# Softmax weights of an attention layer: turned on VectorE and through DRAM in place of TensorE

## The chip, the core and the metric

One core of a Trainium2 chip runs the whole program. The metric is the device time of one execution, in microseconds (us). The core has five engines with a queue of instructions each: TensorE (PE; its weight loads are listed as PEld), VectorE (DVE), ScalarE (ACT), GpSimd (POOL) and SyncE (SP). Here SP does nothing but issue DMAs, and it takes them one after the other: a DMA whose condition isn't met holds up all that stand behind it.

## The reference

Two layers of the same form work on 512 rows of 1024 values. A layer normalises the rows, projects them with one wide matrix, and runs two branches over the result: an attention with 8 heads in 2 groups (compressed keys, selected blocks, window) and a gated linear attention (GLA). Both are scaled by gates, projected up, added, projected out and added to the rows.

```python
s_c = einsum(q_nope, k_cmp) * scale; p_c = masked_softmax(s_c)      # compressed keys
s_s = einsum(q_rope, k_sel) * scale; p_s = masked_softmax(s_s)      # all 8 blocks are selected at 512 rows
s_w = einsum(q_rope, k_win) * scale; p_w = masked_softmax(s_w)      # a window of 512 rows: causal
o   = g0 * (p_c @ v_cmp) + g1 * (p_s @ v_slc) + g2 * (p_w @ v_win)
o   = o * silu(z)
```

With 512 rows the selected blocks and the window both come to plain causal attention over 512 keys, with different keys and values. They are the two branches br = 0 and 1 below.

## The kernel before

Every large product is made from float32 values split in a high and a low part, with three matmuls for each block (lines 158 to 160, called `split3`). The order of TensorE's instructions is that in which the program is written; those of the other engines, and the order of the DMAs in SP's queue, are laid out by the tile framework's scheduler from its own model of the times.

The attention stage of a layer handles four pairs of heads p (head p of each group g = 0, 1). One pair has five steps: the compressed keys (`cmp_steps`), then four `attn_steps(p, ip, br)`. A unit (p, ip, br) covers the 128-row blocks of queries i = 2ip and 2ip + 1. For each i, `scores` makes the two groups' scores (line 775), and `weigh` makes weights of them: VectorE adds the mask and takes the maximum from PSUM (785), ScalarE takes the exponential (787), VectorE the reciprocal (789) and the scaling with the gate (790), into a tile of the pool "g". For i = 0 the scores of both branches are made at once. The product with the values (820) contracts over the keys, so the weights have to be turned first: TensorE transposes each 128x128 block into PSUM (808), three blocks for each group when ip = 0 and seven when ip = 1, and VectorE and ScalarE copy the banks into tiles of the pool "p" (811). The products of a pair all add into one PSUM bank (`ps_o`), which VectorE takes out at 825.

The steps are generators, and a loop written out by hand lays them on TensorE's queue: `go(n)` runs step n to its next yield, and `fill(us)` puts in between that much other work from a queue (the projections, `fm` and `up`), counted at 0.64 us for three matmuls. FILL holds the amounts by n % 5. What is left of the queue after the loop is run by `need("ug7")`; the next stage, `un`, is put in the queue only then.

The projections' weights are read by SP (line 130) into the pool "raw" of three buffers, two tiles ahead of their use, cast on ScalarE (143), and the low part is made on VectorE (144). A read waits until 144 has released a buffer.

Of the kernel before, what the change touches and what calls it, by code (L numbers as in the profile page):

```python
# [1 line left out]

# [1 line left out]

# [5 lines left out]
F32 = mybir.dt.float32  # L10
F32R = mybir.dt.float32r
# [53 lines left out]
def trunk(ctx, tc, x, wpk, sp, gvec, cs, wa, out):  # L65
    nc = tc.nc
    sb = {}

    def pool(name, bufs):
        sb[name] = ctx.enter_context(tc.tile_pool(name=name, bufs=bufs))  # L70
# [2 lines left out]
    pool("hT", 4)  # L73
    pool("hl", 6)
    pool("oT", 16)
    pool("g", 16)
    pool("a", 18)
    pool("raw", 3)
    pool("p", 12)
    pool("th", 2)  # L80
    pool("sm", 4)
    psp = {n: ctx.enter_context(tc.tile_pool(name="ps_" + n, bufs=b, space=PSUM))
# [1 line left out]
    dram = ctx.enter_context(tc.tile_pool(name="dram", bufs=1, space=bass.MemoryType.DRAM))  # L84
    cnt = [0]

    def new(pl, shape=(128, 512), dt=F32, tag=None, bufs=None):
        cnt[0] += 1
        kw = {} if bufs is None else {"bufs": bufs}
        return sb[pl].tile(list(shape), dt, tag=tag or pl, name=f"{tag or pl}_{cnt[0]}", **kw)  # L90

    def ps(tag):
        cnt[0] += 1
        return psp[tag].tile([128, 512], F32, tag=tag, name=f"ps_{tag}_{cnt[0]}")

    def const(shape, dt, name):
        return sb["const"].tile(list(shape), dt, tag=name, name=name)

    mm, tp = nc.tensor.matmul, nc.tensor.transpose
    V, A, G = nc.vector, nc.scalar, nc.gpsimd  # L100
    dma = nc.sync.dma_start


    ident = const((128, 128), F32, "ident")
# [164 lines left out]
    for l in range(L):  # L269
# [20 lines left out]
        def fill(us):  # L290
            credit[0] += us
            while credit[0] > 0.3 and queue:
                credit[0] -= step(*queue[0])
# [9 lines left out]
        def need(name):  # L303
            while name not in done:
                step(*queue[0])


        vsw = [new("a", (128, 2, 256)) for _ in range(2)]
# [63 lines left out]
        b = ps("t")  # L372
# [11 lines left out]
        for t in range(2):  # L384
            o = ps("s")
# [148 lines left out]
        PR = [[None, None, None, None] for _ in range(4)]  # L534
# [98 lines left out]
        def states(t):  # L633
            ub = [ps("s"), ps("s")]
            for n in range(7):
                rows = slice((n % 2) * 64, (n % 2) * 64 + 64)
                s = n // 2
                for r in range(2):
                    h = 2 * t + r
                    mm(ub[n % 2][r * 64:(r + 1) * 64, s * 128:(s + 1) * 128],  # L640
                       khT[t][rows, s * 128 + r * 64:s * 128 + (r + 1) * 64],
                       gv[s][rows, h * 128:(h + 1) * 128], start=True, stop=True)
            stt = [new("g", (128, 4, 128)), new("g", (128, 4, 128))]
            st.append(stt)
            for n in range(1, 8):
                u = ub[(n - 1) % 2][:, ((n - 1) // 2) * 128:((n - 1) // 2 + 1) * 128]
                d_ = stt[n // 4][:, n % 4]
                if n == 1:
                    V.tensor_copy(d_, u)
                else:  # L650
                    V.scalar_tensor_tensor(d_, stt[(n - 1) // 4][:, (n - 1) % 4], dec[t][:, n - 1:n], u,
                                           op0=OP.mult, op1=OP.add)
# [54 lines left out]
        need("gk1")  # L707
        fill(2.0)
        states(0)
        fill(1.0)  # L710
        khat_turn(1)
        fill(2.5)
        intra(0)
        fill(2.5)
        states(1)
        fill(2.5)
        intra(1)
# [41 lines left out]
            mm(acc, vbd[1], pcT, start=False, stop=False, skip_group_check=True)  # L759
            yield  # L760

        pps = {}

        def scores(p, i, brs):

            w = (i + 1) * 128
            ww = w * len(brs)
            both = len(brs) > 1  # L770
            o = [ps("s"), ps("s")]
            for g in range(2):
                for n in range(2):
                    kn = first[g][:, n].rearrange("p b n -> p (b n)") if both else keys[brs[0]][g][n][:, :w]
                    mm(o[g][:, :ww], PR[p][1][g][:, i * 128:(i + 1) * 128], kn, start=(n == 0), stop=(n == 1))  # L775
            for g in range(2):
                weigh(p, g, i, brs, o[g])

        def weigh(p, g, i, brs, o):
            h, w = p + 4 * g, (i + 1) * 128  # L780
            for n, br in enumerate(brs):
                ob = o[:, n * w:(n + 1) * w]
                sx = new("sm", (128, 4), tag="sx", bufs=8)
                pp = new("g")
                V.tensor_tensor_reduce(pp[:, :w], ob, cmask[:, 512 - w:512], 1.0, -3 * NEG,  # L785
                                       OP.add, OP.min, sx[:, 0:1])
                A.activation(pp[:, :w], pp[:, :w], AF.Exp, bias=sx[:, 0:1], scale=-1.0,  # L787
                             accum_out=sx[:, 1:2])
                V.reciprocal(sx[:, 2:3], sx[:, 1:2])
                V.tensor_scalar(pp[:, :w], pp[:, :w], sx[:, 2:3],  # L790
                                gt[:, i, h * 3 + 1 + br:h * 3 + 2 + br], op0=OP.mult, op1=OP.mult)
                pps[p, br, i, g] = pp

        def attn_steps(p, ip, br):
            for i in (2 * ip, 2 * ip + 1):
                if i or not br:
                    scores(p, i, (br,) if i else (0, 1))
                yield

            cols = [(j, i) for j in range(2 * ip + 2) for i in (2 * ip, 2 * ip + 1) if i >= j]  # L800
            pts = []
            for g in range(2):
                pt = []
                for c0 in range(0, len(cols), 4):
                    cc = cols[c0:c0 + 4]
                    bk = ps("t")
                    for n, (j, i) in enumerate(cc):
                        tp(bk[:, n * 128:(n + 1) * 128], pps[p, br, i, g][:, j * 128:(j + 1) * 128], ident)  # L808
                    pt.append(new("p"))
                    w = len(cc) * 128  # L810
                    (A.copy if (g + c0 // 4) % 2 else V.tensor_copy)(pt[-1][:, :w], bk[:, :w])  # L811
                pts.append(pt)
                yield
            acc = PR[p][3]
            for j in range(2 * ip + 2):
                n = cols.index((j, max(j, 2 * ip)))
                w = 256 if j <= 2 * ip else 128
                for g in range(2):
                    c0 = br * 128 + g * 64
                    mm(acc[g * 64:(g + 1) * 64, (2 * ip + 2) * 128 - w:(2 * ip + 2) * 128],  # L820
                       vsw[j // 2][:, j % 2, c0:c0 + 64], pts[g][n // 4][:, n % 4 * 128:n % 4 * 128 + w],
                       start=False, stop=(br == 1 and j == 2 * ip + 1), skip_group_check=True)
            if ip == 1 and br == 1:
                f_ = new("p")
                V.scalar_tensor_tensor(f_, acc, 0.5, PR[p][2], op0=OP.mult, op1=OP.mult)
                H, Lo = new("oT", dt=F32R), new("oT", dt=F32R)
                A.copy(H, f_)  # L827
                G.tensor_tensor(Lo, f_, H.bitcast(F32), op=OP.subtract)  # L828
                oTn[p] = (H, Lo)
            yield  # L830

        steps = []
# [5 lines left out]
        def go(n):  # L838
            if 0 <= n < len(steps):
                next(live[n])  # L840


        for n in range(len(steps) + 2):
            m = n % 5
            f4 = FILL[m]
            if n < len(steps):
                if m == 0:
                    need(f"q{steps[n][0]}")
                if m == 4:
                    need(f"nz{steps[n][0]}")  # L850
            go(n)
            if m in (1, 4):
                go(n - 3)
                go(n - 2)
            fill(f4[0])
            if m != 1:
                go(n - 1)
            fill(f4[1])
            if m != 0:
                go(n)  # L860
                fill(f4[2])
            if m == 2:
                go(n - 2)
            go(n - 1)
            fill(f4[3])
        need("ug7")

# [2 lines left out]
        def take_un(f):  # L870
            def g(th, u):
                t_ = new("p")
                V.scalar_tensor_tensor(t_, th, 1.0, u, op0=OP.add, op1=OP.mult)
                G.tensor_tensor(t_, t_, y2[f], op=OP.add)
                H, Lo = new("g", dt=F32R), new("g", dt=F32R)
                A.mul(H, t_, 0.5)
                V.scalar_tensor_tensor(Lo, t_, 0.5, H.bitcast(F32), op0=OP.mult, op1=OP.subtract)
                yT.append((H, Lo))
            return g
# [13 lines left out]
        for s in range(ST):  # L893
# [4 lines left out]
            o = [ps("s" if s % 2 and n < 2 else "mm") for n in range(len(pieces))]  # L898
# [100 lines left out]
```

## Time and profile before

| | |
|---|---|
| median of 3 runs | 843.58 us (843.55 to 844.6) |
| the profiled execution | 843.52 us, its span 841.7 us |
| TensorE busy | 819.9 us, 97% of the span |
| VectorE busy | 544.4 us, 65% |
| ScalarE busy | 374.9 us, 45% |
| GpSimd busy | 94.9 us, 11% |
| moved by DMA | 82.62 MB |

All times inside the execution are counted from the first instruction of the span. The execution's own time is 1.8 us longer than its span. The attention stage of the first layer lies from 147.0 us (scores of the compressed keys, p = 0) to about 316 us (the last product with the values), that of the second layer from 556.2 us.

### The profile page before, as it was taken

The page shows a single profiled execution, that of the slowest core. Times are in us where ns is not written, and L with a number is a line of the kernel's source. Part 1 is how long each engine was busy: PE and PEld are TensorE (multiplying, and loading weights), DVE is VectorE, ACT ScalarE, POOL GpSimd, SP SyncE. Part 2 cuts the span into 40 slices and gives each one's busy share as a digit, 9 for nine tenths or more (in the row PEclk, how much of TensorE's full clock was granted, in tenths as well). Part 3 has the DMA queues.
Part 4 walks back from the last instruction along what each step waited for, and adds up shares of the span by engine and source line. Part 5 has one row for each costly group of instructions (what it writes and reads, how often), then busy time and mean ns, then how long its engine had stood idle before and what let it go on. Part 6 is the DMA issues. An engine that isn't in the chain of part 4 may idle for free.

```text
span 841.7 us, 12316 instructions
## 1 busy us (share of the span) xinstructions
PE 819.9 (97%) x4570; PEld 676.8 (80%) x4570; DVE 544.4 (65%) x1192; ACT 374.9 (45%) x775; POOL 94.9 (11%) x118
## 2 busy tenths in 40 slices
PE   4999999999999999999999999999999999999996
PEld 3888788888888878888898878887888888788886
DVE  5653749987776755655564465699877767366322
ACT  4681236564544544443256412555554545244211
POOL 3110033001000001121010001410100000112100
PEclk9999999999999999999999999999999999999999
DMA  8432124221122123546246121332121212255321
GB/s 287 163 135 78 51 67 122 75 70 51 52 63 66 60 63 101 165 157 221 72 136 210 50 76 51 104 96 78 51 63 52 63 51 64 75 154 160 125 100 51
DMA packets 31515, 82.62 MB, mean 98 GB/s; under 512 B 4032, under 2 KB 4576, under 8 KB 31456
## 3 DMA queue, kind: packets, MB, share of 16 engines
q1 hardware_dynamic: 31456, 81.84, 31.1%
q8 instruction: 36, 0.59, 0.3%
q14 instruction: 23, 0.19, 0.1%
HBM read 74.48 MB, written 4.19 MB: 93 GB/s over the span
## 4 chain that ended last, share of the span: by engine, by line
PE 92%; DVE 4%; issue 2%; DMA 1%; SPq 1%; POOL 0%; POOLq 0%; ACT 0%; DVEq 0%; ACTq 0%
PE ps_mm L158 22%; PE ps_mm L160 21%; PE ps_mm L159 21%; PE ps_o L820 4%; PE ps_s L775 4%; PE ps_t L808 4%; PE ps_mm L905 2%; PE ps_mm L906 2%; PE ps_mm L908 2%; PE ps_s L908 1%; PE ps_s L905 1%; PE ps_s L906 1%; DVE a L452 1%; PE ps_mm L467 1%; PE ps_t L207 1%
## 5 line engine op out<-in xcount | busy, mean ns | idle before, releaser
L158 PE MATMUL ps_mm<-hT,hl 128*128 128x512 f32 x544 | 221.2, 407 | 0.0
L159 PE MATMUL ps_mm<-hT,hl 128*128 128x512 f32 x544 | 212.8, 391 | 0.0
L160 PE MATMUL ps_mm<-hT,hl 128*128 128x512 f32 x544 | 212.5, 391 | 0.0
L143 ACT CAST hl<-raw 128x1024 fp32r<-128x1024 f32 (+3 forms) x110 | 100.5, 915 | 145.0 <-PE ps_mm L159 105.1
L144 DVE TENSOR_TENSOR hl<-raw,hl 128x1024 fp32r<-128x1024 f32 (+3 forms) x109 | 128.2, 1178 | 48.3 <-ACT hl L143 46.5
L160 PEld LDWEIGHTS ps_mm<-hT,hl 128*128 128x128 f32 x544 | 102.2, 188 | 22.6
L158 PEld LDWEIGHTS ps_mm<-hT,hl 128*128 128x128 f32 x544 | 102.3, 188 | 20.7 <-issue 2.1
L159 PEld LDWEIGHTS ps_mm<-hT,hl 128*128 128x128 f32 x544 | 102.5, 188 | 17.7
L787 ACT ACTIVATE g<-g,sx 128x128 f32<-128x128 f32 (+3 forms) x128 | 70.8, 554 | 66.9 <-DVE sx L785 66.4
L785 DVE CUSTOM_DVE_ANT_0 g<-ps_s,cmask 128x128 f32<-128x128 f32 (+3 forms) x128 | 57.5, 487 | 28.9 <-PE ps_s L775 28.6
L790 DVE TENSOR_SCALAR g<-g,sx,gt 128x128 f32<-128x128 f32 (+3 forms) x128 | 57.7, 461 | 2.8
L158 PE MATMUL ps_mm<-oT,hl 128*128 128x512 f32 x128 | 52.7, 412 | 0.0
L159 PE MATMUL ps_mm<-oT,hl 128*128 128x512 f32 x128 | 50.1, 391 | 0.0
L160 PE MATMUL ps_mm<-oT,hl 128*128 128x512 f32 x128 | 50.0, 391 | 0.0
L808 PEld LDWEIGHTS ps_t<-ident,g 128*128 128x128 f32 x320 | 38.7, 140 | 9.6 <-DVE g L790 1.4
L775 PE MATMUL ps_s<-a,a 128*128 128x256 f32 (+2 forms) x224 | 46.4, 329 | 0.0
L808 PE MATMUL ps_t<-ident,g 128*128 128x128 f32 x320 | 45.7, 272 | 0.7 <-DVE g L790 0.7
L775 PEld LDWEIGHTS ps_s<-a,a 128*128 128x128 f32 x224 | 38.3, 188 | 6.0
L181 POOL TENSOR_TENSOR rs<-ms,mhalf 128x1 f32<-128x1 f32 (+1 forms) x24 | 17.7, 738 | 205.0 <-DVE ms L179 201.1
L811 ACT COPY p<-ps_t 128x384 f32<-128x384 f32 (+1 forms) x48 | 24.4, 507 | 34.2 <-PE ps_t L808 34.0
L828 POOL TENSOR_TENSOR oT<-p,oT 128x512 fp32r<-128x512 f32 x8 | 12.4, 1555 | 240.6 <-ACT oT L827 240.6
L820 PE MATMUL ps_o<-p,a 128*64 128x256 f32 (+1 forms) x384 | 38.1, 348 | 0.0
(225 smaller groups left out, 1343.5 us busy)
## 6 DMA issues: line engine op xcount, KB each, us to landing
raw<-wpk SPq DMA_DIRECT2D x96, 512.0 KB, 3.5
raw<-wpk SPq DMA_DIRECT2D x32, 256.0 KB, 2.7
a<-wpk SPq DMA_DIRECT2D x16, 256.0 KB, 4.6
p<-x SPq DMA_DIRECT2D x16, 256.0 KB, 4.0
g<-x SPq DMA_DIRECT2D x8, 256.0 KB, 5.5
p<-gvec SPq DMA_DIRECT2D x8, 256.0 KB, 6.0
p<-a SPq DMA_DIRECT2D x32, 64.0 KB, 2.0
x<-p SPq DMA_DIRECT2D x8, 256.0 KB, 2.0
```

The costliest lines, as they stand in the source:

```text
L143: A.copy(H[:, :w], r[:, :w])
L144: (G if i == 1 else V).tensor_tensor(Lo[:, :w], r[:, :w], H[:, :w].bitcast(F32), op=OP.subtract)
L158: mm(o, w[0], h[0], start=first, stop=False)
L159: mm(o, w[0], h[1], start=False, stop=False)
L160: mm(o, w[1], h[0], start=False, stop=last)
L775: mm(o[g][:, :ww], PR[p][1][g][:, i * 128:(i + 1) * 128], kn, start=(n == 0), stop=(n == 1))
L785: V.tensor_tensor_reduce(pp[:, :w], ob, cmask[:, 512 - w:512], 1.0, -3 * NEG, OP.add, OP.min, sx[:, 0:1])
L787: A.activation(pp[:, :w], pp[:, :w], AF.Exp, bias=sx[:, 0:1], scale=-1.0, accum_out=sx[:, 1:2])
L790: V.tensor_scalar(pp[:, :w], pp[:, :w], sx[:, 2:3], gt[:, i, h * 3 + 1 + br:h * 3 + 2 + br], op0=OP.mult, op1=OP.mult)
L808: tp(bk[:, n * 128:(n + 1) * 128], pps[p, br, i, g][:, j * 128:(j + 1) * 128], ident)
L820: mm(acc[g * 64:(g + 1) * 64, (2 * ip + 2) * 128 - w:(2 * ip + 2) * 128], vsw[j // 2][:, j % 2, c0:c0 + 64], pts[g][n // 4][:, n % 4 * 128 ...
L905: mm(o[n][:, :c1 - c0], yy[0], wo[k][h][0][:, c0:c1], start=(k == 0), stop=False)
```

## The change

The transposes on TensorE and the copies out of PSUM go. In their place, `turn` has VectorE transpose the weights in blocks of 32x32, one instruction for each i and group, into a tile T of 128 x 4 x r values (r = 192 for ip = 0 and 448 for ip = 1, so 384 KB and 896 KB). When both i of a unit are there, the tile is written to DRAM by one DMA and read back by four, each of which puts a quarter onto 32 partitions of a tile W. The products take their moving operand from W, in runs of 32 values. T has one buffer for each ip, W two. Each unit's write is ordered behind the last read of the unit before in SP's queue. The pools "g" and "p" lose four buffers each; the GLA states and three of the pairs that `un` makes live in the buffers of W and T.

The products with the values move later: those of ip = 0 from the next steps to the end of step m = 4 (m = n % 5), those of ip = 1 from the start of the next pair's m = 1 to the start of its m = 2. The loop has one more turn at its end. FILL is unchanged.

```diff
-    pool("g", 16)
+    pool("g", 12)
-    pool("p", 12)
+    pool("p", 8)
+    pool("T", 1)
+    pool("PT", 2)
...
-            stt = [new("g", (128, 4, 128)), new("g", (128, 4, 128))]
+            both = new("PT", (128, 2, 4, 128), tag="PT1")
+            stt = [both[:, 0], both[:, 1]]
...
+        PT, TT, held, back = {}, {}, {}, []
+        def turn(p, br, i, pps):
+            ip, n = i // 2, i + 1
+            r = (4 * ip + 3) * 64
+            if i % 2 == 0:
+                TT[p, br] = new("T", (128, 4, r), tag=f"T{ip}")
+            T = TT[p, br]
+            t = T[:, :, (i % 2) * i * 64:((i % 2) * i + n) * 64].rearrange("p b (j g q) -> p b j g q", j=n, g=2)
+            for g in range(2):
+                V.transpose(t[:, :, :, g], pps[g][:, :n * 128].rearrange("p (j b q) -> p b j q", j=n, b=4))
+            if i % 2:
+                cnt[0] += 1
+                dr = dram.tile([128, 4, r], F32, tag=f"tp{ip}", name=f"tp_{cnt[0]}", bufs=2)
+                with tc.issue_after(back[-1]) if back else nullcontext():
+                    dma(dr, T)
+                W = PT[p, br, ip] = new("PT", (128, 4, r), tag=f"PT{ip}")
+                for b in range(4):
+                    back.append(dma(W[b * 32:(b + 1) * 32], dr[:, b].rearrange("(a k) r -> k a r", a=4)).ins)
...
-            cols = [(j, i) for j in range(2 * ip + 2) for i in (2 * ip, 2 * ip + 1) if i >= j]
...
-                        tp(bk[:, n * 128:(n + 1) * 128], pps[p, br, i, g][:, j * 128:(j + 1) * 128], ident)
...
-                    (A.copy if (g + c0 // 4) % 2 else V.tensor_copy)(pt[-1][:, :w], bk[:, :w])
...
+                    if j <= i0:
+                        m = W[:, :, :2 * (i0 + 1) * 64].rearrange("p a (i j g q) -> p i a j g q", i=2, g=2, q=32)
+                        m, w = m[:, :, :, j, g], 256
+                    else:
+                        m, w = W[:, :, (2 * j) * 64 + g * 32:(2 * j) * 64 + g * 32 + 32], 128
...
-        for n in range(len(steps) + 2):
+        for n in range(len(steps) + 3):
...
             go(n)
-            if m in (1, 4):
+            if m == 2:
+                go(n - 4)
                 go(n - 3)
-                go(n - 2)
             fill(f4[0])
-            if m != 1:
+            if m == 1:
                 go(n - 1)
             fill(f4[1])
...
             if m == 2:
                 go(n - 2)
-            go(n - 1)
+            if m == 4:
+                go(n - 3)
+                go(n - 2)
             fill(f4[3])
...
-                H, Lo = new("g", dt=F32R), new("g", dt=F32R)
+                if f < 3:
+                    both = new("PT", (128, 2, 512), F32R, tag="PT1") if f < 2 else new("T", (128, 2, 512), F32R, tag="T1")
+                    H, Lo = both[:, 0], both[:, 1]
+                else:
+                    H, Lo = new("g", dt=F32R), new("g", dt=F32R)
```

## Rows read from the trace of the kernel before

**Rows 1.** The page's busy times (part 1) and its chain of waits (part 4).

```profile
span 841.7 us, 12316 instructions
PE 819.9 (97%) x4570; PEld 676.8 (80%) x4570; DVE 544.4 (65%) x1192; ACT 374.9 (45%) x775; POOL 94.9 (11%) x118
...
PE 92%; DVE 4%; issue 2%; DMA 1%; SPq 1%; POOL 0%; POOLq 0%; ACT 0%; DVEq 0%; ACTq 0%
```

**Rows 2.** Windows of layer 0's attention: length, busy us per engine, clock, DMA share, GB/s.

```profile
147.00:182.80 35.80, 35.47 (x192) 29.10 (x190) 33.22 (x90) 21.26 (x52) 2.59 (x2) 1.00 0.25 70
182.80:223.80 41.00, 41.00 (x241) 33.37 (x241) 32.14 (x94) 21.63 (x55) 3.21 (x2) 1.00 0.20 58
223.80:264.70 40.90, 40.90 (x241) 33.31 (x241) 30.88 (x91) 20.49 (x51) 1.81 (x1) 1.00 0.20 59
264.70:303.00 38.30, 38.30 (x225) 31.29 (x225) 26.82 (x82) 17.96 (x45) 1.81 (x1) 1.00 0.21 62
303.00:316.00 13.00, 13.00 (x86) 10.22 (x85) 6.12 (x14) 4.07 (x9) 0.00 (x0) 1.00 0.21 62
```

**Rows 3.** Timeline of TensorE around seven transposes: start, duration, instruction.

```profile
218.11 0.39 PE L159 MATMUL ps_mm<-oT,hl 128*128 128x512 f32 x1
218.34 0.40 PE L160 MATMUL ps_mm<-oT,hl 128*128 128x512 f32 x1
218.57 0.93 PE L808 MATMUL ps_t<-ident,g 128*128 128x128 f32 x7
219.25 0.48 PE L158 MATMUL ps_mm<-oT,hl 128*128 128x512 f32 x1
```

**Rows 4.** Groups of instructions by line and shape: busy us, mean ns, idle before.

```profile
L808 PE MATMUL ps_t<-ident,g 128*128 128x128 f32 x320 | 45.7, 272 | 0.7 <-DVE g L790 0.7
...
L785 DVE CUSTOM_DVE_ANT_0 g<-ps_s,cmask 128x512 f32<-128x512 f32 x32 | 20.8, 687 | 1.8 <-PE ps_s L775 1.6
...
L785 DVE CUSTOM_DVE_ANT_0 g<-ps_s,cmask 128x384 f32<-128x384 f32 x32 | 16.6, 554 | 11.4 <-PE ps_s L775 11.4
...
L785 DVE CUSTOM_DVE_ANT_0 g<-ps_s,cmask 128x256 f32<-128x256 f32 x32 | 12.4, 420 | 8.0 <-PE ps_s L775 8.0
...
L785 DVE CUSTOM_DVE_ANT_0 g<-ps_s,cmask 128x128 f32<-128x128 f32 x32 | 7.8, 286 | 7.7 <-PE ps_s L775 7.7
```

**Rows 5.** The five windows of rows 2 for line 811 alone: their sum.

```profile
sum 169.00, DVE 14.29 ACT 12.18; mean DVE 2.86 ACT 2.44
```

**Rows 6.** DMA issues (part 6): size of one, median us from issue to landing.

```profile
raw<-wpk SPq DMA_DIRECT2D x96, 512.0 KB, 3.5
raw<-wpk SPq DMA_DIRECT2D x32, 256.0 KB, 2.7
...
p<-a SPq DMA_DIRECT2D x32, 64.0 KB, 2.0
```

**Rows 7.** Line 506 (DMAs onto 32 partitions) in SP's queue: ns min/median/max of one issue.

```profile
L506 SPq DMA_DIRECT2D p<-a x32: 512/586/1526, 136.1 to 600.6; - x32
```

**Rows 8.** Timeline of TensorE at the end of layer 0's attention.

```profile
301.89 1.07 PE L775 MATMUL ps_s<-a,a 128*128 128x512 f32 x4
...
312.05 3.25 PE L820 MATMUL ps_o<-p,a 128*64 128x256 f32 x32
...
316.72 0.39 PE L158 MATMUL ps_mm<-hT,hl 128*128 128x512 f32 x1
```

**Rows 9.** The chain of waits in order of time: the last products of ip = 0.

```profile
296.87 1.45 PE ps_o L820 x16
```

**Rows 10.** Timeline of VectorE: the last scaled weights of layer 0.

```profile
305.64 0.99 DVE L790 TENSOR_SCALAR g<-g,sx,gt 128x512 f32<-128x512 f32 x2
```

**Rows 11.** Timeline of TensorE: last scores of p = 1, first transposes of p = 2.

```profile
220.03 1.07 PE L775 MATMUL ps_s<-a,a 128*128 128x512 f32 x4
...
241.49 0.49 PE L808 MATMUL ps_t<-ident,g 128*128 128x128 f32 x3
```

**Rows 12.** What SP's queue waited for: us in total, times, longest.

```profile
SPq L130 <- DVE hl L144: 384.0, 75, 18.4
```

More of the change, by code (lines that the diff above doesn't have):

```diff
@@ L1 @@
-from contextlib import ExitStack
+from contextlib import ExitStack, nullcontext
 import numpy as np
@@ L760, in cmp_steps @@
             yield
-        pps = {}
+        PT, TT, held, back = {}, {}, {}, []
[16 more added lines that the diff above has]
+                    back.append(dma(W[b * 32:(b + 1) * 32], dr[:, b].rearrange("(a k) r -> k a r", a=4)).ins)
         def scores(p, i, brs):
@@ L775, in scores @@
                     mm(o[g][:, :ww], PR[p][1][g][:, i * 128:(i + 1) * 128], kn, start=(n == 0), stop=(n == 1))
-            for g in range(2):
-                weigh(p, g, i, brs, o[g])
+            pps = [weigh(p, g, i, brs, o[g]) for g in range(2)]
+            turn(p, brs[0], i, [t[0] for t in pps])
+            if both:
+                held[p] = [t[1] for t in pps]
         def weigh(p, g, i, brs, o):
             h, w = p + 4 * g, (i + 1) * 128
+            out = []
             for n, br in enumerate(brs):
@@ L791, in weigh @@
                                 gt[:, i, h * 3 + 1 + br:h * 3 + 2 + br], op0=OP.mult, op1=OP.mult)
-                pps[p, br, i, g] = pp
+                out.append(pp)
+            return out
         def attn_steps(p, ip, br):
@@ L797, in attn_steps @@
                     scores(p, i, (br,) if i else (0, 1))
+                else:
+                    turn(p, br, i, held.pop(p))
                 yield
-            cols = [(j, i) for j in range(2 * ip + 2) for i in (2 * ip, 2 * ip + 1) if i >= j]
[L801 to L807, printed above, removed]
-                        tp(bk[:, n * 128:(n + 1) * 128], pps[p, br, i, g][:, j * 128:(j + 1) * 128], ident)
-                    pt.append(new("p"))
-                    w = len(cc) * 128
-                    (A.copy if (g + c0 // 4) % 2 else V.tensor_copy)(pt[-1][:, :w], bk[:, :w])
[L812 to L817, printed above, removed]
+            acc, W = PR[p][3], PT[p, br, ip]
+            i0 = 2 * ip
+            for j in range(i0 + 2):
                 for g in range(2):
                     c0 = br * 128 + g * 64
-                    mm(acc[g * 64:(g + 1) * 64, (2 * ip + 2) * 128 - w:(2 * ip + 2) * 128],
-                       vsw[j // 2][:, j % 2, c0:c0 + 64], pts[g][n // 4][:, n % 4 * 128:n % 4 * 128 + w],
-                       start=False, stop=(br == 1 and j == 2 * ip + 1), skip_group_check=True)
+                    if j <= i0:
[3 more added lines that the diff above has]
+                        m, w = W[:, :, (2 * j) * 64 + g * 32:(2 * j) * 64 + g * 32 + 32], 128
+                    mm(acc[g * 64:(g + 1) * 64, (i0 + 2) * 128 - w:(i0 + 2) * 128],
+                       vsw[j // 2][:, j % 2, c0:c0 + 64], m,
+                       start=False, stop=(br == 1 and j == i0 + 1), skip_group_check=True)
             if ip == 1 and br == 1:
@@ L874, in g @@
                 G.tensor_tensor(t_, t_, y2[f], op=OP.add)
-                H, Lo = new("g", dt=F32R), new("g", dt=F32R)
+                if f < 3:
+                    both = new("PT", (128, 2, 512), F32R, tag="PT1") if f < 2 else new("T", (128, 2, 512), F32R, tag="T1")
+                    H, Lo = both[:, 0], both[:, 1]
+                else:
+                    H, Lo = new("g", dt=F32R), new("g", dt=F32R)
                 A.mul(H, t_, 0.5)
@@ L990 @@
     arrays = {k: np.ascontiguousarray(v) for k, v in _layout(inputs).items()}
-    nc = _bacc.Bacc("TRN2", target_bir_lowering=False, num_devices=1)
+    nc = _bacc.Bacc("TRN2", target_bir_lowering=False, num_devices=1, dynamic_dma_scratch_size=1024)
     args = [nc.dram_tensor(n, arrays[n].shape, mybir.dt.from_np(arrays[n].dtype), kind="ExternalInput").ap()
```

## The prediction

> **What bounds the kernel now.** I read the busy times first. TensorE is busy for 97% of the span, and the chain of waits that ended last runs through it for 92% [rows 1]. A busy TensorE need not be full, so I cut the first layer's attention stage into its four pairs of heads and the end. In these windows TensorE has no gap at all but 0.3 us in the first, at a granted clock of 1.00 [rows 2]: every instruction taken off its queue there shortens the stage, as long as nothing else becomes late. What could become late stands in the same rows: VectorE is busy for 33.2 of 35.8 us in the first pair, for 26.8 to 32.1 us in the others, and for 129.2 of 169.0 us in all five windows. The DMA engines are at a quarter of their time or less.
>
> **TensorE's share.** A transpose's own row says 272 ns, but they overlap [rows 4]. What one is worth is read from the timeline. The matmul ahead of a group of seven ends at 218.34 + 0.40 = 218.74, the one behind it at 219.25 + 0.48 = 219.73. That one matmul is worth 0.23 us, the distance of the two starts ahead (218.11, 218.34) [rows 3], so the seven took 0.99 - 0.23 = 0.76 us, 0.109 each. For 320 of them it is **34.9 us** off the queue, 17.4 in each layer. The stretch of rows 2 would fall from 169.0 to 151.6 us if TensorE stayed full. The products with the values keep their number and columns. Their operand now comes in runs of 32 values; no row shows such a read. It can hardly gain, as the columns stay, and if it ran at half speed it would cost the products' own time once more: 1.45 us for a pair's ip = 0 and 3.25 for its ip = 1 [rows 8, 9], 4.7 x 8 = 38 us. I take nothing, since no column is added.
>
> **VectorE's share.** Copies out of PSUM go: 14.3 us in the stretch [rows 5]. ScalarE's copies go too, 12.2 us, and give nothing, since ScalarE was half idle. In their place come 64 transposes in a layer, 16 of each width from 128 to 512. None is in the trace. The nearest row by shape and rate is the masking at line 785, which passes one value a step: 286, 420, 554 and 687 ns [rows 4]. 16 x 1.947 = 31.2 us. Lower end: the cost of a wide one grows half as fast, 24.7 us; upper end: every 128-column block pays the price of a 128-wide instruction, 160 x 0.286 = 45.8 us. I take 31.2, since the width has a clear slope in the rows. Then VectorE's work in the stretch is 129.2 - 14.3 + 31.2 = 146.1 us. That is under TensorE's 151.6, but the most that VectorE has reached in a window of this stage is 33.2 / 35.8 = 0.93 [rows 2], as it also waits inside each softmax for ScalarE. At 0.93, 146.1 us of work need 157.4 us. VectorE, not TensorE, then sets the stretch: 5.8 us of the gain are given back in each layer, **11.6 us** in all. TensorE feels it where the next scores want the two PSUM banks that line 785 reads.
>
> The page "VectorE: DVE Perf Modes" of the Trainium skill (The three transpose paths) gives 311 ns for a 128x128 transpose in bf16 on VectorE against 390 ns on TensorE, and its rules tell to use TensorE for a 128x128 block. The trace disagrees about TensorE: 0.109 us in a row of seven. By 311 ns for each of 160 blocks, an estimate from that page, VectorE's work would be 164.7 us, and the time about 867 us.
>
> **The way through DRAM.** It is on no engine's busy time, but it makes a latency where a PSUM copy stood. From the last scores of a layer (301.89 + 1.07 = 302.96) to the scaled weights (305.64 + 0.99 = 306.63) pass 3.7 us [rows 8, 10]; two transposes add 1.4; the write of 896 KB takes 4.7, which is 3.5 for 512 KB and 0.8 for each 256 KB more [rows 6]; four reads are issued in 4 x 0.586 = 2.3 us [rows 7], and the last, 224 KB, lands about 2.6 later by the 256 KB row. Lower end: the last read lands like one of 64 KB, in 2.0; upper end: four reads that don't overlap, 4 x 2.7 = 10.8. Sum: **14.7 us**, 14 to 21; I take the overlap, as issues here follow each other without waiting for the landing.
>
> Against it stands the work on TensorE's queue ahead of the product. For p = 0 to 2, from the end of the last scores (221.1) to the start of the next pair's step m = 2, which is one fill of 1.2 ahead of 241.49, so about 240.2 [rows 11]: 19.1 us. Three groups of transposes leave it (2.3), the ip = 1 products move behind (3.2), the ip = 0 products move in (1.45): 15.0, and branch 0's product, whose weights come earlier, adds 1.6. 16.6 us cover 14.7. So nothing, with 1.9 us to spare; without the cover it is microsecond for microsecond, three times a layer.
>
> The last pair has no such cover. Behind the last products of before only 1.4 us of the filler remain (315.30 to 316.72, where the next stage's first tile starts), and the next stage isn't in the queue yet [rows 8]. The lead is 312.05 - 302.96 = 9.1, less 2.3 for the transposes, plus 1.45, plus 1.4, plus 1.6 for branch 0: 11.2 us against 14.7. TensorE stands for 3.5 us in each layer, **7.0 us** in all, and VectorE has nothing to catch up with then, so it adds to the 11.6.
>
> **The queues.** SP's queue holds each unit's write, and then its four reads, which wait until the write has landed; a weight read behind them is held for about 4.7 + 2.3 = 7.0 us, 24 to 28 us in a pair of some 37. Two tiles of lead are more than 10 us of TensorE's work, so I take nothing, and rival D prices it. ACT's and POOL's queues get nothing. The added traffic is 42 MB; in a pair 5.2 MB on some 37 us, 140 GB/s beside 60, about two thirds of what the present 0.20 at 58 GB/s comes to at full share [rows 2]. The buffers: the states and the pairs of the next stage leave the pool "g" by as many tiles as it loses, and "p" loses the turned weights' tiles. At the end of layer 0 the squares may wait for a group of transposes, at most some 0.8 us three times; I take nothing.
>
> **Sum.** The profiled execution's 843.52 us (1.8 over its span, 0.06 under the median) - 34.9 + 11.6 + 7.0 = **827 us**.
>
> **The rivals.**
> B, *VectorE keeps up.* Its 146.1 us are under 151.6, and the products now wait long enough to take a lag of some us. For it: TensorE no longer needs the weights at once. Against: in the first pair VectorE is at 33.2 of 35.8 us already [rows 2], and would get work while TensorE loses some. It gives 843.5 - 34.9 + 7.0 = 816 us, 809 if the end is covered too.
> C, *VectorE becomes the bound outright.* Price: 45.8 us of transposes in a layer, 160.7 us of work, 173.1 at 0.93, plus 3.5; against 169.0 it is 7.6 us lost in each layer: 859 us, **slower**. It decides at (169.0 - 3.5) x 0.93 - 114.9 = 39 us, 0.61 us for the mean transpose, where I took 0.49. Against it: the slope with the width.
> D, *the strict queue.* SP's weight reads wait 384 us in 75 cases for a buffer, 5.1 us each and up to 18.4 [rows 12]. If one stands ahead of the last unit's write or reads, the way takes 19.8 us: 3.2 us missing three times and 8.6 at the end, 18.2 in each layer. 843.5 - 34.9 + 36.4 = 845 us, 857 if VectorE's 11.6 come on top; I put it at 850. Against it: buffers and turned weights are both released by VectorE, in one order.
> E, *the operand in runs of 32 is slow to read.* Up to 38 us on top, 865; I give it little, as the reads' columns are unchanged.
>
> **Chances.** The forecast 0.49 (818 to 840 by itself: 25 to 36 us of transposes, 0 to 7 us at each end), B 0.22, C 0.11, D 0.13, E 0.05. What this kernel's measurement tells from no change is about 0.2%, 1.7 us. Faster holds the forecast, B and a little of D: 0.71; same 0.05; slower 0.24. The range leaves out C and E and the lower edge of B: 812 to 851 us.
>
> **What would show it.** Right: no line 808, TensorE's instructions in the stage less by 160 a layer, VectorE at 0.9 or more of the attention windows, transposes of 0.29 to 0.69 us, and one gap of 3 to 4 us ahead of the last line of products in each layer, ended by a DMA into W. B: VectorE with gaps in the first pair, TensorE full. C: transposes over 0.6 us. D: SP's queue waiting at line 130 for VectorE while T is done, and gaps ahead of the products in every pair. E: the products longer than 1.45 and 3.25 us with their operands there. The forecast falls if the stage's gaps lie elsewhere, in the projections' tiles above all (weights that come late), or if the GLA stage shows gaps that were not there.

## The result, and the profile after

The changed kernel takes **850.54 us** (median of 4 runs, 847.07 to 852.23) against 843.57 us for the kernel before on the same chip. The ratio is 1.0074, interval 1.0058 to 1.0091: 0.7% slower. The forecast was 827.0 us, so faster: the direction is missed, and the value lies just inside the upper end of the range of 812 to 851 us.

The profiled execution took 847.07 us, the fastest of the four. First its page: busy times, the groups at the changed lines, and the DMA issues (KB each, median us to landing).

```profile
span 845.0 us, 11999 instructions
PE 792.1 (94%) x4250; PEld 647.3 (77%) x4250; DVE 560.0 (66%) x1272; ACT 352.7 (42%) x727; POOL 94.6 (11%) x118
...
L840 PE MATMUL ps_o<-PT,a 128*64 128x256 f32 (+1 forms) x384 | 42.9, 368 | 21.3 <-DMA PT<-tp 21.3
...
tp<-T SPq DMA_DIRECT2D x16, 896.0 KB, 4.5
PT<-tp SPq DMA_DIRECT2D x64, 224.0 KB, 4.8
tp<-T SPq DMA_DIRECT2D x16, 384.0 KB, 2.6
PT<-tp SPq DMA_DIRECT2D x64, 96.0 KB, 2.2
```

Against [rows 1], TensorE has 320 instructions less and is busy for 27.8 us less (819.9 to 792.1). What is left of the span grows from 841.7 - 819.9 = 21.8 to 845.0 - 792.1 = 52.9 us, by 31.1. So 27.8 us were saved and 31.1 were spent waiting. Where TensorE waits stands in its waits (us in total, times, longest):

```profile
PE ps_o L840 <- DMA PT<-tp: 21.3, 8, 6.6
PE ps_s L799 <- DVE sx L812: 4.8, 4, 1.9
PE ps_t L755 <- DVE g L751: 2.7, 3, 0.9
PE ps_t L755 <- ACT g L814: 1.9, 1, 1.9
```

The first line is the products with the values, which wait for weights on their way back from DRAM: eight times, once in every pair of heads. The second is the scores, which wait for VectorE to leave a PSUM bank. The last two are the transposes of the compressed keys' weights (755), which still stand on TensorE. Before, the four pairs and the end of layer 0 held 0.33 us without TensorE in all [rows 2]. The other stages didn't change: at equal matmuls the two kernels are 0.64 us apart where layer 0's attention begins and 0.07 us where it has ended, and within 0.02 us of that through the next stage. In the second layer they go from 0.52 us apart where the attention begins to 3.22 where it has ended: 2.7 of the 3.3 us by which the span is longer are lost there, to waits of the same kinds and one more stretch at the lower clock.

The same five windows of layer 0's attention as in [rows 2], shifted to the pairs as they lie now:

```profile
147.60:183.20 35.60, 32.93 (x167) 26.37 (x165) 34.34 (x98) 19.68 (x48) 2.59 (x2) 1.00 0.42 129
183.20:221.90 38.70, 36.87 (x201) 29.36 (x201) 34.72 (x105) 19.04 (x47) 3.56 (x2) 1.00 0.70 208
221.90:261.20 39.30, 36.57 (x200) 29.18 (x199) 33.13 (x101) 17.73 (x46) 1.30 (x1) 1.00 0.67 199
261.20:299.50 38.30, 37.16 (x203) 29.88 (x203) 31.95 (x98) 16.98 (x44) 1.30 (x1) 1.00 0.66 197
299.50:316.60 17.10, 10.55 (x58) 7.43 (x56) 5.44 (x11) 2.17 (x3) 0.00 (x0) 0.80 0.79 221
```

The first pair gains almost nothing: VectorE is busy for 34.34 of 35.6 us. The second and third gain 2.3 and 1.6 us, where the 40 transposes of a pair are worth 4.4; the fourth gains nothing, and the end gets 4.1 us longer, at a mean granted clock of 0.80. The sum is 169.0 us, as before.

Two ways through DRAM in layer 0, from the timeline (start, duration, instruction; in brackets, how long the engine stood ahead of it and what ended that): the second pair's last unit, and the layer's last.

```profile
217.19 1.08 PE L799 MATMUL ps_s<-a,a 128*128 128x512 f32 x4
225.38 0.70 DVE L778 STREAM_TRANSPOSE T<-g 128x512 f32<-128x512 f32 x1
226.11 0.34 SPq L783 DMA_DIRECT2D tp<-T  x1
226.54 1.44 SPq L132 DMA_DIRECT2D raw<-wpk  x2
230.75 1.75 SPq L786 DMA_DIRECT2D PT<-tp  x4
237.84 1.73 PE L840 MATMUL ps_o<-PT,a 128*64 128x256 f32 x16 [1.84 <-DMA PT<-tp]
...
294.29 1.12 PE L799 MATMUL ps_s<-a,a 128*128 128x512 f32 x4
301.03 1.30 DVE L778 STREAM_TRANSPOSE T<-g 128x512 f32<-128x512 f32 x2
302.36 0.34 SPq L783 DMA_DIRECT2D tp<-T  x1
302.80 1.33 SPq L132 DMA_DIRECT2D raw<-wpk  x2
305.20 1.74 PE L840 MATMUL ps_o<-PT,a 128*64 128x256 f32 x16
306.97 1.75 SPq L786 DMA_DIRECT2D PT<-tp  x4
313.49 3.20 PE L840 MATMUL ps_o<-PT,a 128*64 128x256 f32 x16 [6.55 <-DMA PT<-tp]
316.62 0.50 PE L160 MATMUL ps_mm<-hT,hl 128*128 128x512 f32 x1
```

In the first, the scores end at 218.27, the transposes at 226.08, the write is issued at 226.11, the first read at 230.75 and the last by 232.50, and the product starts at 237.84. The way takes 19.6 us and is 1.84 us late. In the second it is 295.41, 302.33, 302.36, 306.97, 308.72 and 313.49: 18.1 us, 6.55 us late. The late product then takes 3.20 us for 16 matmuls where the punctual one ahead took 1.74. The granted clock says why:

```profile
310.00:317.00 7.00, 3.51 (x18) 2.26 (x19) 0.28 (x1) 0.00 (x0) 0.00 (x0) 0.54 0.47 104
```

In this window it is 0.54: TensorE ran at about the lower of its two levels, after having stood since 306.94. The kernel before shows such a stretch only behind its last matmuls. The change has three ahead of them, at 0.50: two at the ends of the layers (309.67 to 316.50 and 722.68 to 729.51), and one in the second layer's first pair:

```profile
575.91:579.33 3.42, 3.42 (x9) 2.76 (x9) 3.42 (x11) 0.55 (x3) 0.00 (x0) 0.50 0.42 115
```

TensorE is busy for 10.6 us of the three, which at half the clock is some 5.3 us of lost time.

### The profile page after: what moved, and what is told of

It is laid out like the page before. It is cut to its first block, busy times and chain, and to the rows that moved or that the text cites. A ratio compares the mean times of both kernels' runs of the same rounds, so it can differ in the third digit from the quotient of the medians.

```text
span 845.0 us, 11999 instructions
## 1 busy us (share of the span) xinstructions
PE 792.1 (94%) x4250; PEld 647.3 (77%) x4250; DVE 560.0 (66%) x1272; ACT 352.7 (42%) x727; POOL 94.6 (11%) x118
## 5 line engine op out<-in xcount | busy, mean ns | idle before, releaser
L778 DVE STREAM_TRANSPOSE T<-g 128x256 f32<-128x256 f32 (+3 forms) x128 | 61.2, 497 | 13.2 <-DMA tp<-T 12.6
L840 PE MATMUL ps_o<-PT,a 128*64 128x256 f32 (+1 forms) x384 | 42.9, 368 | 21.3 <-DMA PT<-tp 21.3
L840 PEld LDWEIGHTS ps_o<-PT,a 128*64 128x64 f32 x384 | 27.8, 144 | 38.0 <-issue 26.3
L799 PE MATMUL ps_s<-a,a 128*128 128x256 f32 (+2 forms) x224 | 48.3, 334 | 4.9 <-DVE sx L812 4.8
L161 PE MATMUL ps_mm<-oT,hl 128*128 128x512 f32 x128 | 50.0, 391 | 0.0
L160 PE MATMUL ps_mm<-oT,hl 128*128 128x512 f32 x128 | 50.0, 390 | 0.0
L162 PE MATMUL ps_mm<-oT,hl 128*128 128x512 f32 x128 | 49.8, 389 | 0.0
L848 POOL TENSOR_TENSOR oT<-p,oT 128x512 fp32r<-128x512 f32 x8 | 10.4, 1296 | 248.1 <-ACT oT L847 248.1
L896 POOL TENSOR_TENSOR p<-p,g 128x512 f32<-128x512 f32 x16 | 25.4, 1589 | 107.7 <-DVE p L895 96.2
```

Source lines behind the costliest of these rows:

```text
L160: mm(o, w[0], h[0], start=first, stop=False)
L161: mm(o, w[0], h[1], start=False, stop=False)
L162: mm(o, w[1], h[0], start=False, stop=last)
L778: V.transpose(t[:, :, :, g], pps[g][:, :n * 128].rearrange("p (j b q) -> p b j q", j=n, b=4))
L840: mm(acc[g * 64:(g + 1) * 64, (i0 + 2) * 128 - w:(i0 + 2) * 128], vsw[j // 2][:, j % 2, c0:c0 + 64], m, start=False, stop=(br == 1 and j = ...
```

## The experiments

The theory after the result: the exchange of engines itself does what was forecast, and the time went into the way through DRAM, which is longer than the work put ahead of the products. The rivals: VectorE as the bound, the transposes at 755, one buffer too few for the tile T, and the queue of SP.

The table gives every kernel's time with its ratio to the kernel before, and from its profiled execution TensorE's busy time and the rest of the span. After the change all have the same 4250 matmuls, so a larger busy time means that they are slower, or that more of them stand beside a gap, where nothing covers their ends.

| kernel | us, median | ratio (interval) | PE busy | rest |
|---|---|---|---|---|
| before | 843.58 | 1 | 819.9 | 21.8 |
| the change | 850.54 | 1.0074 (1.0058 to 1.0091) | 792.1 | 52.9 |
| c_notrip | 821.32 | 0.9736 (0.9713 to 0.9759) | 784.7 | 33.0 |
| b_act | 833.02 | 0.9869 (0.9853 to 0.9884) | 790.0 | 40.4 |
| a_tail | 842.98 | 0.9988 (0.9973 to 1.0003) | 794.0 | 49.2 |
| g_cmp | 845.57 | 1.0026 (1.0007 to 1.0045) | 790.8 | 49.5 |
| t_two | 847.39 | 1.0031 (1.0013 to 1.0049) | 792.7 | 51.1 |
| e_late | 833.33 | 0.9868 (0.9852 to 0.9883) | 789.8 | 40.5 |
| f_both | 831.07 | 0.9837 (0.9816 to 0.9859) | 796.4 | 34.0 |
| f2_pool | 833.73 | 0.9872 (0.9857 to 0.9886) | 795.1 | 36.4 |
| k_gates | **824.63** | 0.9771 (0.9754 to 0.9789) | 790.3 | 31.0 |

**c_notrip: the way through DRAM left out.** VectorE transposes as in the change, and the products read its tile directly. The turn of the four groups of 32 keys, which the DMAs do, is left out.

```diff
-                TT[p, br] = new("T", (128, 4, r), tag=f"T{ip}")
+                TT[p, br] = new("PT", (128, 4, r), tag=f"PT{ip}")
...
-                with tc.issue_after(back[-1]) if back else nullcontext():
-                    dma(dr, T)
-                W = PT[p, br, ip] = new("PT", (128, 4, r), tag=f"PT{ip}")
-                for b in range(4):
-                    back.append(dma(W[b * 32:(b + 1) * 32], dr[:, b].rearrange("(a k) r -> k a r", a=4)).ins)
+                PT[p, br, ip] = T
```

> VectorE's transposes stay, the write and the four reads go: the products read the tile that the transposes wrote (so the weights are turned in 32x32 blocks only, and the products are taken with those). Theory (latency of the way through DRAM): all waits ahead of line 840 go, some 4 us in the first three pairs and 8 at the end of each layer with the half clock; 824 to 830 us. Waits of the scores for VectorE (2.7 and 2.0 us) and of the compressed keys' transposes (1.8 and 2.8) stay. Rival (VectorE's 32 us of transposes per layer are what costs): only the end's 8 us per layer go, 834 us or more, and the waits move to the scores.

Measured 821.32 us, 29.2 us under the change, and 2.7 under the theory's range of 824 to 830. On the page, the product has the mean duration that it had before, 348 ns, though it reads the same runs of 32 values as in the change.

```profile
PE 784.7 (96%) x4250; PEld 643.3 (79%) x4250; DVE 557.5 (68%) x1272; ACT 353.3 (43%) x727; POOL 93.8 (11%) x118
...
L834 PE MATMUL ps_o<-PT,a 128*64 128x256 f32 (+1 forms) x384 | 38.1, 348 | 0.0
```

Its waits of TensorE in the attention:

```profile
PE ps_s L793 <- DVE sx L806: 7.3, 4, 2.2
PE ps_t L755 <- DVE g L751: 2.8, 4, 0.9
```

Only those for VectorE are left. TensorE's busy time is 819.9 - 784.7 = 35.2 us less than before, and the rest 33.0 - 21.8 = 11.2 us more. In size these are the forecast's first two terms, 34.9 and 11.6; what the second is made of comes below. Layer 0's attention, from 147.60 to 304.70 us, has this sum:

```profile
sum 157.10, PE 151.81 PEld 121.16 DVE 138.83 ACT 75.98 POOL 8.00; mean PE 30.36 PEld 24.23 DVE 27.77 ACT 15.20 POOL 1.60
```

The way through DRAM adds 27.3 us of span to this kernel: 19.9 of waiting (52.9 - 33.0) and 7.4 of TensorE's busy time (792.1 - 784.7). Of these 7.4 the lower clock explains 5.3, as this kernel has no such stretch ahead of its last matmuls. The other 2 or so fit what the gaps leave uncovered: 16 products take 1.73 us at the upper level, and 32 without a gap between them 3.25, not 3.46.

**b_act: VectorE relieved.** ScalarE copies the weights into T in place of VectorE's transposes; the turn inside the 32x32 blocks is left out, all transfers stay.

```diff
-                V.transpose(t[:, :, :, g], pps[g][:, :n * 128].rearrange("p (j b q) -> p b j q", j=n, b=4))
+                A.copy(t[:, :, :, g], pps[g][:, :n * 128].rearrange("p (j b q) -> p b j q", j=n, b=4))
```

> The same way through DRAM, but ScalarE copies the weights into T instead of VectorE turning them (the weights are not turned within the blocks). VectorE has 32 us less in each layer, ScalarE about as much more of the time it has free. Theory (latency): within 4 us of 850, as the waits ahead of line 840 are set by the write and the reads, of 4.6 and 6.5 us. Rival (VectorE): the scores' waits for VectorE and those of the compressed keys go, and the way begins earlier; 6 to 10 us per layer, 832 to 840 us.

Measured 833.02 us, 17.5 under the change. The waits of the scores and of line 755 are gone, and what the products wait is nearly what it was:

```profile
PE ps_o L840 <- DMA PT<-tp: 18.0, 8, 6.2
```

So the transfers delay the products with VectorE relieved as well. But the time is in the rival's range (832 to 840 us), not within 4 us of 850 as the theory had it: the change also loses by VectorE's load. This kernel doesn't part VectorE's price from that of the way, since the softmax ahead of each way gets shorter too.

**a_tail: work behind the last products.** The next stage's first block, un0, goes into the filler's queue before the loop, in place of behind it (its products hold back until the attention's output is there).

```diff
+                while src[k] is None:
+                    yield 9.0
...
+        put("un0", up(0, "mgn", "un", oTn, take_un(0)))
         for n in range(len(steps) + 3):
...
-        for f in range(8):
+        for f in range(1, 8):
```

> The next stage's first tile is put in the filler's queue ahead of the loop, so that TensorE has some 7 us of work (8 groups of its gate, 3 of its product) while the last unit of a layer comes back from DRAM; nothing else changes. Theory (the way through DRAM is longer than the work left at the end of a layer): the two gaps of 6.3 and 6.6 us ahead of the last products all but go, with them the two stretches at half clock that begin in them; 6 to 8 us per layer, 834 to 838 us against 850.5. Rival (VectorE is the bound, and the gap only shows its backlog): the last unit comes later by as much as work is put ahead of it, the gap stays over 4 us, the time above 845.

Measured 842.98 us: 7.6 us gained where 12 or more were expected, between the theory's time and the rival's. The gap at the end fell from 6.55 only to 4.28 us, since the loop's fill amounts let only 12 matmuls of the new work, 2.7 us, go ahead of the last products. Those still ran slowly:

```profile
317.44 2.80 PE L842 MATMUL ps_o<-PT,a 128*64 128x256 f32 x16 [4.28 <-DMA PT<-tp]
```

**g_cmp: line 755 back in its old place.** The change had also moved the transposes of the compressed keys' weights, from the end of step m = 1 to behind its first fill.

```diff
             fill(f4[0])
-            if m == 1:
-                go(n - 1)
             fill(f4[1])
             if m != 0:
                 go(n)
                 fill(f4[2])
+            if m == 1:
+                go(n - 1)
```

> One place in the loop: the transposes of the compressed keys' weights go back to the end of step m = 1; the products stay where the change put them. Theory (of the 17 us that the run with both moves gained, the products' leads are the larger part): the four waits at those transposes go, 4.6 us, and the waits ahead of line 840 stay: 844 to 848 us. Rival (that place is what cost, as it holds up everything behind it): 836 to 840 us.

Measured 845.57 us, 5.0 gained, as the theory had it. Line 755 no longer waits; the products wait as much as before (23.3 us in 8 cases, against 21.3).

**t_two: a second buffer for T of ip = 0.** VectorE stood for this tile's write to DRAM 12.6 us in four cases.

```diff
-    pool("g", 12)
+    pool("g", 11)
...
-                TT[p, br] = new("T", (128, 4, r), tag=f"T{ip}")
+                TT[p, br] = new("T", (128, 4, r), tag=f"T{ip}", bufs=2 - ip)
```

> The changed kernel with two buffers instead of one for the tile that VectorE transposes the weights of ip = 0 into (and one buffer less in the pool g, which makes the room). Theory (part of what makes the products late is VectorE standing for this tile's write to DRAM, 12.6 us in 4 cases, 2.6 to 4.3 each, all in pairs behind the first): these waits go, the waits ahead of the products of the middle pairs shrink by 1 to 2 us a layer, the end of a layer stays as it is; 846 to 849 us. Rival (the tile's second buffer only lets VectorE run ahead of a transfer that the products wait for anyway, or the missing buffer of g holds VectorE instead): the wait is gone or moves, the time stays within 1 us of the changed kernel's 850.5.

Measured 847.39 us, 3.2 gained. VectorE's wait is gone, but the products' waits hardly change (19.2 us in 8 cases). The time is the theory's, the waits are nearer the rival's; about a tenth of what the way costs goes with this edit.

**e_late: later places for the products.** The products of ip = 1 go from the start of the next pair's step m = 2 to its end, the third part of `cmp_steps` from there to m = 3, and line 755 back as in g_cmp. Nothing else.

```diff
-            if m == 2:
-                go(n - 4)
-                go(n - 3)
             fill(f4[0])
-            if m == 1:
-                go(n - 1)
+            if m == 3:
+                go(n - 3)
             fill(f4[1])
             if m != 0:
                 go(n)
                 fill(f4[2])
+            if m == 1:
+                go(n - 1)
             if m == 2:
-                go(n - 2)
+                go(n - 4)
+                go(n - 3)
```

> Only places in the loop change: the products of ip = 1 stand at the end of step m = 2 and not at its start (some 4 us later), the start of a pair's products at m = 3, and the compressed keys' transposes at the end of m = 1, where they stood before the change. Theory (leads that are too short): the waits ahead of line 840 in the first three pairs (3.9 and 4.6 us per layer) and those of the compressed keys (1.8 and 2.8) go, the end of a layer stays: 838 to 843 us. Rival (VectorE is the bound): the waits reappear at the scores, 847 us or more.

Measured **833.33 us**: 17.2 us gained, faster than both kernels, by places alone, and more than the theory's 838 to 843. Of the products' eight waits two are left, the ends of the layers:

```profile
PE ps_o L840 <- DMA PT<-tp: 11.9, 2, 6.4
```

**f_both: e_late and a_tail together.** 

> Both edits together: the products of ip = 1 and the compressed keys' transposes later, and the next stage's first tile in the filler's queue, of which the loop's last turn can now use some 5.5 us ahead of the last products. Theory (the cost of the way through DRAM is leads that are too short, each of them by itself): the gaps of 6.4 and 5.5 us at the ends fall under 1.5 us, no half clock is left there; 817 to 822 us, as without the way through DRAM (821.3). Rival (the added tile's weights crowd the DMA engines while the last unit comes back, as the first run with the tile alone gained 7.5 us of 16): gaps of 3 us and more, 824 to 829 us.

Measured 831.07 us, not 817 to 822, and above the rival's 824 to 829 too. No product waits any more: the rest of the span is 34.0 us, within 1.0 of the kernel that has no way at all. But un0's last matmuls now stand directly behind the attention, whose result still has to go through VectorE, ScalarE and GpSimd:

```profile
315.38 0.80 PE L160 MATMUL ps_mm<-oT,hl 128*128 128x512 f32 x1 [2.45 <-ACT oT L849]
316.73 0.80 PE L161 MATMUL ps_mm<-oT,hl 128*128 128x512 f32 x1 [0.55 <-POOL oT L850]
```

The two waits are 3.0 us, and the windows (the number ahead of the DMA share is the granted clock) show the rest of the price:

```profile
312.00:315.30 3.30, 0.94 (x5) 0.41 (x3) 1.89 (x3) 1.73 (x3) 0.00 (x0) 1.00 0.03 12
315.30:322.10 6.80, 6.17 (x14) 4.50 (x15) 2.21 (x3) 1.70 (x3) 3.48 (x2) 0.50 0.42 116
```

TensorE was idle for most of the first window; through the whole second one, in which it is busy again for 6.17 of 6.8 us, it has the lower level. Over the execution the same matmuls take 796.4 - 784.7 = 11.7 us more than in c_notrip, more than in any other kernel here. There are four such stretches ahead of the last matmuls, with 19.2 us of busy time, so some 9.6 of the 11.7 are the clock.

**f2_pool: f_both with less on VectorE.** The low parts of three weights go to GpSimd.

```diff
-        (G if i == 1 else V).tensor_tensor(Lo[:, :w], r[:, :w], H[:, :w].bitcast(F32), op=OP.subtract)
+        (G if i == 1 or n in ("nz0", "q2", "nz1") else V).tensor_tensor(Lo[:, :w], r[:, :w], H[:, :w].bitcast(F32), op=OP.subtract)
```

> As the run with both edits, and the low parts of three tiles of weights that fall in the first pair's time are made on GpSimd instead of VectorE, 1.2 to 1.4 us each. Theory (in the first pair VectorE is the bound, which the scores' waits of 1.9 and 0.9 us show): these waits shrink, 3 to 6 us under the run with both. Rival (GpSimd is slow at it and slows VectorE's accesses): the weights come late, no gain or up to 10 us more.

Measured 833.73 us: no gain, the rival's time. The scores' waits for VectorE grew from 3.9 us in two cases to 6.9 in four. The trace shows both halves of the rival in the first pair (the third line is the same scaling, of the other group):

```profile
157.90 2.40 POOL L146 TENSOR_TENSOR hl<-raw,hl 128x1024 fp32r<-128x1024 f32 x1
158.22 2.23 DVE L819 TENSOR_SCALAR g<-g,sx,gt 128x256 f32<-128x256 f32 x1
160.85 0.37 DVE L819 TENSOR_SCALAR g<-g,sx,gt 128x256 f32<-128x256 f32 x1
```

GpSimd needs 2.40 us for what VectorE did in 1.2, and a scaling on VectorE that begins meanwhile takes 2.23 us in place of 0.37. The second layer shows the same at 563.19.

**k_gates: independent work between the products and what needs them.** From f_both, `up` is cut in its gate tile, which doesn't need the attention, and its products. The gate tiles of two blocks are queued ahead of the products, and the weights are read in that order.

```diff
             yield from fm(l, f"{gate}{f}", hT, sig)
+            if src is not oTn or f > 1:
+                yield from prod(f, wn, src, then, th)
+            gated[f] = th
...
+        def prod(f, wn, src, then, th=None):
+            th = th or gated[f]
...
-        put("un0", up(0, "mgn", "un", oTn, take_un(0)))
+        for f in range(2):
+            put(f"gate{f}", up(f, "mgn", "un", oTn, take_un(f)))
+        for f in range(2):
+            put(f"un{f}", prod(f, "un", oTn, take_un(f)))
```

> The late places of e_late, and the gate tiles of the next stage's first two blocks on TensorE's queue ahead of their products with the attention's output, so that one gate tile (24 matmuls, some 5 us) stands between the last products with the values and the first matmul that needs them. Theory (after f_both what is left at the end of a layer is the wait for the output chain on VectorE, ScalarE and GpSimd, 2.45 + 0.55 us, and the half clock behind it): both waits go, no stretch at half clock near the end of a layer, 819 to 824 us. Rival (the weights of the next stage come late because SP's reads stand behind the turned weights): the wait reappears ahead of the gate tiles or of line 160, ended by the weights, and the time stays at 828 to 832 us. What stays by both: the waits of the scores for VectorE, 2 to 3 us a layer.

Measured **824.63 us**, 2.3% under the kernel before and the fastest of those that leave nothing out. Neither of the waits for the attention's output is left, and little of the others:

```profile
PE ps_o L851 <- DMA PT<-tp: 3.9, 2, 2.4
PE ps_s L810 <- DVE sx L823: 3.9, 2, 1.9
PE ps_s L810 <- DVE g L754: 1.6, 2, 0.8
```

The time is just above the theory's 819 to 824, and not every step of it came: the last product of a layer still waits (1.56 and 2.35 us), and short stretches at half clock stay (from about 165.5, 565 and 708 us).

## Why the prediction was wrong

The forecast was a gain of 16.5 us, and the change lost 7.0. The exchange of engines brought about what was forecast; what failed is the price of the way through DRAM, 7.0 us in the sum and 29.2 measured.

**TensorE's share, 34.9 us: right.** With the way left out the busy time falls by 35.2. The worth of a transpose read from the row of seven [rows 3], 0.109 us, held, and not its own 272 ns. The page "VectorE: DVE Perf Modes" of the Trainium skill (Rules for kernel authors) would leave 128x128 blocks to TensorE. c_notrip, which leaves out the turn of the four groups, shows the exchange of engines by itself to be worth 22.3 us where TensorE is the bound, although a block costs 0.19 us on VectorE (61.3 us for 320) and 0.109 on TensorE.

**VectorE's transposes, 31.2 us a layer: right.** The groups by form:

```profile
L778 DVE STREAM_TRANSPOSE T<-g 128x512 f32<-128x512 f32 x32 | 21.5, 691 | 0.0
L778 DVE STREAM_TRANSPOSE T<-g 128x384 f32<-128x384 f32 x32 | 17.4, 563 | 0.0
L778 DVE STREAM_TRANSPOSE T<-g 128x256 f32<-128x256 f32 x32 | 14.2, 443 | 0.4
L778 DVE STREAM_TRANSPOSE T<-g 128x128 f32<-128x128 f32 x32 | 8.3, 290 | 12.7 <-DMA tp<-T 12.6
```

16 x 1.987 = 31.8 us; the masking's rows [rows 4] were the right neighbours, and rival C is out.

**VectorE as the bound, 11.6 us: right in size, only partly in its way.** c_notrip measures 821.32 - (843.58 - 34.9) = 12.6 by the medians; at equal matmuls each of its two attentions is 12.7 us shorter than before, where the forecast had 17.4 - 5.8 = 11.6. But VectorE's work in layer 0's is 138.8 us, not 146.1, and 138.8 at 0.93 would need 149.6, less than TensorE's 151.6: by the forecast's own rule VectorE would have taken nothing back. VectorE is the bound in the first pair only, where the scores wait for it (7.3 us in both layers together). Another 2.8 us are waits at line 755, for work of VectorE too, in a place where the forecast had no wait. That the whole comes near 11.6 is in part luck. Rival B, in which VectorE keeps up, is out.

**The operand in runs of 32: right at nothing.** The product has 348 ns in c_notrip as before. Rival E is out.

**The way through DRAM, 7.0 us: wrong.** It costs 850.54 - 821.32 = 29.2 us. The step that failed is "So nothing, with 1.9 us to spare", with the 3.5 us at the end that came of the same sum: the products wait 21.3 us in all, 8.4 of them in the pairs, where nothing was taken, and 12.9 at the two ends, where 7.0 were. The lead was read well: 17.7 us in the second pair (218.27 to the 236.00 at which TensorE was free), 16.6 forecast; at the end 11.5 (295.41 to 306.94), 11.2 forecast. The write was right too, 4.6 us for 4.7. Two terms of the way were too small:

- From the scores to the last transpose: 5.1 us forecast, 7.8 in the second pair and 6.9 at the end. The 3.7 us came from the kernel before, where VectorE had time. The forecast itself made VectorE the bound of this stage, yet took the softmax at its old speed. In b_act, with VectorE relieved, the same part, up to the last copy into T, takes 6.3 and 4.5 us.
- From the last read's issue to the product: 2.6 us forecast, 5.3 and 4.8 measured. The 2.6 is the landing of one such DMA in the kernel before, at a DMA share of 0.2; four reads of 224 KB at once, beside weight reads, land in 4.8 by the median, at a share of 0.7. The forecast had itself put the load in a pair at about two thirds of the full share, yet took the landing from rows at 0.2.

With issues 0.55 us shorter than forecast, the way is 18.1 to 19.6 us against 14.7. That turns a spare 1.9 into waits of 0.92 to 1.84 us in the pairs, and 3.5 into 6.55 at the end. Which it is that makes the reads slow, that there are four of them or that weight reads run beside them, stays open: it wasn't tried.

**What the sum didn't hold.** First, the clock: of the 27.3 us of span between c_notrip and the change, some 5.3 are matmuls at the lower level, 3.6 of them at the ends of the layers. A gap was priced at its own length. Second, line 755: the diff moves it, the prediction followed only the products, and its move costs 5.0 us. Third, the single buffer of T, costed at nothing: about 3 us went with it in t_two.

**Rival D, the strict queue: right in its time, wrong in its mechanism.** It gave 850 us, by chance. In both timelines above SP has issued its weight reads some 2.8 us before the turned weights' reads can go, which wait for the write itself, and the weight reads wait less for buffers than before (248.7 us in 63 cases; [rows 12] has 384 in 75). The ordering line (782) binds nothing: without it the program has the same instructions in the same order in every queue.

## What to carry to other kernels

When a step leaves the busiest engine and gets a long latency in return, the gain is paid out only if the work ahead of its consumer is longer than the whole latency, measured with the new load on the engines and queues that it passes; here a spare of 1.9 us by the old load's rows was gone under the new one. Then look one step on: what first depends on the late result needs its own cover, as f_both and k_gates show. The same exchange was 0.7% slower, or 1.3% to 2.3% faster once its products and the work around them had other places (e_late, k_gates), so before giving up a change of engines, move its consumers.

## What the hardware showed that I had not expected

A wait of a few microseconds on TensorE can cost about twice its length. In f_both a wait of 2.45 us at the end of layer 0 was followed by 6.8 us at a granted clock of 0.50 (with the second wait, 0.55 us, inside them), in which matmuls that stand 0.227 us apart at the upper level stood 0.43 us apart: so some 3 us more. It doesn't follow every wait of the same length. TensorE waits 1.94 to 1.95 us for the same scores in the first pair of each layer in five kernels: in e_late the clock stays at 1.00 both times, in a_tail, f_both and k_gates it falls both times, and in the change it stays in the first layer and falls in the second (575.91 us). What decides this no run here shows. In c_notrip no wait of the attention, up to 2.24 us, is followed by a fall. The page "TensorE: Matmul & The Clock Gate" of the Trainium skill (Part 1: The HAM clock gate) puts the penalty of the ramp at under 1% of a typical kernel's span; it speaks there of a kernel's first matmuls. The stretches here come in mid-kernel, behind waits, and cost some 9.6 of 830.4 us, 1.2%, in f_both, and 5.3 of 845.0, 0.6%, in the change.

A VectorE instruction that has begun can be held up beside one of GpSimd. In f2_pool a scaling that takes 0.37 us elsewhere took 2.23 beside GpSimd's subtraction of 2.40 and ended 0.15 us behind it, in both layers. In the kernel before, a scaling at line 790 took 1.47 us beside a GpSimd instruction of 1.30 (at 154.96 us). That the one causes the other is read from these coincidences; no run sets them apart.
